# Hybrid SSD / RWKV-7 block on one core: high and low activations in one 512-column matmul of the input projection, rows normalised before the transposes

## The chip, the core and the metric

The kernel runs on one core of a Trainium2 chip. The core has a matmul engine (TensorE, PE in the profile; its weight loads are PEld) and four others that work beside it: VectorE (DVE), ScalarE (ACT), GpSimd (POOL) and the queue engine SyncE (SP), which here only issues DMAs. Each engine works through its own instructions in order, and semaphores make one wait for another. Matmuls write to PSUM, a small accumulation memory that the kernel uses as eight banks, each with room for 128 partitions x 512 f32; DVE and ACT read it from there. The metric is the time of one execution on the device, in microseconds (us).

## The reference

One layer of a streaming encoder block for 256 frames of 2048 channels, everything float32:

```python
u = rms_norm(h, norm1_g)                     # u = h * rsqrt(mean(h*h)) * g, by row (frame)
P = u @ w_in                                 # 2048 x 11744: z | x,B,C of the SSD | dt | r,k,v,wd,ad,gd of RWKV-7
pr = pr + (prev(pr) - pr) * rwkv_mu          # token shift: mixes each frame with the one before
y_ssd  = ssd_mixer(z, silu(conv4(xbc)), dt)  # Mamba-2, chunks of 64 frames
y_rwkv = rwkv7_mixer(r, k, v, wd, ad, gd)    # 32 heads of 64
h = h + concat(y_ssd, y_rwkv) @ w_out
v = rms_norm(h, norm2_g)
h = h + (silu(v @ w_gate) * (v @ w_up)) @ w_down      # D_FF = 5632
out = rms_norm(h, norm_f_g)
```

## The kernel before

**Products in three parts.** Every large product of float32 matrices is made of three faster ones. `split` turns a weight tile `raw` into a rounded high part `whi` (ACT, line 192) and the rest `wlo` (DVE, line 193); the activations have a high part `uh` and a low part `ul` in the same way. A product is then whi·uh + whi·ul + wlo·uh, added up in PSUM.

**Two kinds of product.** `gemm_a` makes 256 output channels x 256 frames with the weights as the stationary operand and the activations as the moving one: 16 slices of the 2048 input channels, two halves `b` of 128 output channels, and three matmuls of 256 columns for each (lines 277, 278, 279), 96 in all. It serves the low-rank inputs (`ps_l0`, `ps_l1`), r, k and v of eight RWKV pairs of 256 channels (`ps_rkv`, 24 calls), B and C (`ps_bc`, 4) and x of the SSD (`ps_xs`, 8): 38 calls. `gemm_b` turns the operands round: the activations are stationary and 512 weight columns move (lines 298 to 300). It serves z, the output projection (`add_out`, `ps_o`) and the FFN.

**PSUM.** Pool `mm` has four buffers of one bank for the results of both kinds; a `gemm_a` takes one, a `gemm_b` two (one for each half of the frames). Pool `mx`, four further banks, serves everything small. A buffer is given again only when the instructions that read its last result are done.

**Normalisation.** The raw x is transposed (line 247) and scaled by the norm weights into `uh`, `ul` (lines 252, 254). The factor of each frame, `rstd`, is not yet known then. It is worked out beside that (`square`, `finish`), spread over all partitions as a row `R` by a matmul (`row_scale`), and each `gemm_a` result is multiplied by R afterwards, in PSUM (`scaled`, line 231, DVE). z gets the factor in its activation. At the start the four quarters of x and the four weight tiles of `ps_l0` are loaded in turn, and the function `first` makes transposes, splits and matmuls quarter by quarter.

**After each gemm_a.** For r, k, v the function `shift` reads each half `j` of the scaled result twice: line 353 (ACT) writes a part to SBUF, line 354 (DVE) adds the frame before. B, C and x go through `conv` (line 877 on ACT, three times line 879 on DVE).

**Order.** Work beside the large products is put into a queue with due times (`Side`; one tick for each weight tile), and the framework's scheduler then places the instructions of each engine by priority, so the order on the engines is fixed at build time. The loop over the eight pairs makes k, v and r of pair `pi`, while the side queue has the recurrence of the two pairs before; then, from pair 3 on, `out_rwkv` multiplies the finished pair `pi - 3` with its 256 rows of the output projection: `add_out`, four column blocks n0 to n3 of 12 matmuls each, and each block is added to `h` by two DVE additions (line 311). B and C follow, then the output of pair 5, then four SSD groups g0 to g3 (two `ps_xs`, an `add_out` of another pair or group, one `ps_z` each), the last outputs, and the FFN, which takes the time from about 1112 us on.

Of the kernel before, what the change touches and what calls it, by code (L numbers as in the profile page):

```python
# [68 lines left out]
def tile_hybrid_block(ctx: ExitStack, tc: tile.TileContext, x, norm1_g, w_in, conv_w, conv_b, dt_bias, A_log, D_skip,  # L69
# [12 lines left out]
    mm = ctx.enter_context(tc.tile_pool(name="mm", bufs=4, space=PS))  # L82
# [5 lines left out]
    def mmt(name):  # L88
        return mm.tile([P, 2, T], F32, name=name, tag="mm")
# [23 lines left out]
    for _ in range(10):  # L113
        nc.tensor.matmul(ps[:, :P], ones, ones, start=True, stop=True)
# [81 lines left out]
    uh = ul = R = None  # L196
# [20 lines left out]
    def row_scale(i, pool):  # L217

        nonlocal R
        ps = mxt("ps_R")  # L220
        for b in range(2):
            r = finish(i, b)
            dg = pool.tile([P, P], F32, name="diag_r")
            nc.vector.tensor_scalar(dg, ident, r, None, ALU.mult)
            nc.tensor.matmul(ps[:, b * P:(b + 1) * P], ones, dg, start=True, stop=True)
        R = const.tile([P, T], F32, name="R")
        nc.scalar.copy(R, ps[:, :T])

    def scaled(ps):

        nc.vector.tensor_tensor(ps, ps, R.unsqueeze(1).broadcast_to([P, 2, T]), ALU.mult)
        return ps

    def to_channels(n, gcol, order=lambda ins: ins):

        nonlocal uh, ul
        if n == 0:
            uh = big.tile([P, KT, T], F32R, name="uh")
            ul = big.tile([P, KT, T], F32R, name="ul")
        tiles = []  # L240
        for k2 in range(2):
            ps = mxt("ps_n").rearrange("p (a t) -> p a t", a=2)
            tiles.append(ps)
            for b in range(2):
                for j in range(2):
                    c = n * 512 + (2 * k2 + j) * P
                    order(nc.tensor.transpose(out=ps[:, j, b * P:(b + 1) * P], in_=h[:, b, c:c + P], identity=ident))

        def half(k2):
            ks = [(4 * n + 2 * k2 + j, tiles[k2][:, j]) for j in range(2)]  # L250
            for k, ps in ks:
                order(nc.scalar.activation(uh[:, k], ps, AF.Copy, scale=gcol[:, k:k + 1]))
            for k, ps in ks:
                order(nc.vector.scalar_tensor_tensor(ul[:, k], ps, gcol[:, k:k + 1], uh[:, k].bitcast(F32), ALU.mult,
                                                     ALU.subtract))

        return half
# [9 lines left out]
    def gemm_a(w, cols, name, units=None):  # L267
        ps = mmt(name)
        for k0 in range(0, KT, 4):
            hi, lo = split(load_a(w, cols, k0)) if units is None else units(k0 // 4)  # L270
            for k in range(4):
                kt = k0 + k
                first, last = kt == 0, kt == KT - 1
                for b in range(2):
                    o = ps[:, b]
                    wh, wl = hi[:, k, b * P:(b + 1) * P], lo[:, k, b * P:(b + 1) * P]
                    nc.tensor.matmul(o, wh, uh[:, kt], start=first and b == 0, stop=False)  # L277
                    nc.tensor.matmul(o, wh, ul[:, kt], start=False, stop=False)  # L278
                    nc.tensor.matmul(o, wl, uh[:, kt], start=False, stop=last and b == 1)  # L279
            side.tick()  # L280
        return ps

    def gemm_b(w, r0, c0, acts, name):

        ps = [mmt(name).rearrange("p a t -> p (a t)") for _ in range(2)]
# [31 lines left out]
    cols = [(0, 256, CGD)]  # L317
    raws, halves = [], []
# [3 lines left out]
    halves.append(to_channels(0, colN, pin))  # L322

    def first(n):
        halves[n](0)
        hi_lo = split(raws[n], pin)
        halves[n](1)
        if n < 3:
            halves.append(to_channels(n + 1, colN, pin))
        for b in range(2):  # L330
            square(0, init, b, n, ("act", "vec")[b], pin)
        return hi_lo

    ps_l0 = gemm_a(w_in, cols, "ps_l0", first)
    row_scale(0, init)
# [32 lines left out]
    ps = scaled(ps_l0)  # L368
# [488 lines left out]
    for pi in range(8):  # L857
# [23 lines left out]
    for i in range(4):  # L881
        ps = scaled(gemm_a(w_in, [(0, 256, CXBC + 2048 + i * 256)], "ps_bc"))
        if i == 0:
# [3 lines left out]
            BC = bcp.tile([P, 2, 4, T], F32, name="BC")  # L887
        for j in range(2):
# [112 lines left out]
    uacts = [(uh[:, k], ul[:, k]) for k in range(KT)]  # L1001
    for g in range(4):
        xc = []
        for i in range(2):
            ps = scaled(gemm_a(w_in, [(0, 256, CXBC + g * 512 + i * 256)], "ps_xs"))
            t = xz.tile([P, 2, T], F32, name="xc", tag=f"xc{i}")
            for j in range(2):
                conv(t[:, j], ps[:, j], 4 * g + 2 * i + j)
# [8 lines left out]
        for b in range(2):  # L1017
            nc.scalar.activation(zs[:, b], psz[b], AF.Silu, scale=rstd[0][:, b:b + 1])
# [11 lines left out]
    def after(b, n):  # L1030
        square(1, npool, b, n, ("act", "vec")[b])
        if b == 1:
            half = to_channels(n, colB[:, N2:N2 + KT])
# [13 lines left out]
    uacts = [(uh[:, k], ul[:, k]) for k in range(KT)]  # L1047
# [97 lines left out]
```

## Time and profile before

| | |
|---|---|
| Runs | 1672.49, 1672.7 and 1674.29 us; median 1672.7 |
| Profiled execution | 1674.88 us, span of its instructions 1673.2 us, granted TensorE clock 0.999 |
| PE busy | 1654.7 us (99%), 12386 matmul records |
| PEld busy | 1440.8 us (86%) |
| DVE busy | 1196.1 us (71%) |
| ACT busy | 892.7 us (53%) |
| First matmul of `ps_l0`, of the first `ps_rkv` | 9.71 us, 37.81 us |

Busy time is a sum over stages. In the RWKV stage (37.8 to about 600 us) DVE is nearly as busy as PE; in the FFN PE stands alone. A difference of 2 us in 1674 between the profiled execution and the median is what separate executions of this kernel differ by (the runs above span 1.8 us).

### The profile page before, as it was taken

The page shows a single profiled execution, that of the slowest core. Times are in us where ns is not written, and L with a number is a line of the kernel's source. Part 1 is how long each engine was busy: PE and PEld are TensorE (multiplying, and loading weights), DVE is VectorE, ACT ScalarE, POOL GpSimd, SP SyncE. Part 2 cuts the span into 40 slices and gives each one's busy share as a digit, 9 for nine tenths or more (in the row PEclk, how much of TensorE's full clock was granted, in tenths as well). Part 3 has the DMA queues.
Part 4 walks back from the last instruction along what each step waited for, and adds up shares of the span by engine and source line. Part 5 has one row for each costly group of instructions (what it writes and reads, how often), then busy time and mean ns, then how long its engine had stood idle before and what let it go on. Part 6 is the DMA issues. An engine that isn't in the chain of part 4 may idle for free.

```text
span 1673.2 us, 30550 instructions
## 1 busy us (share of the span) xinstructions
PE 1654.7 (99%) x12386; PEld 1440.8 (86%) x12386; DVE 1196.1 (71%) x1859; ACT 892.7 (53%) x1390; POOL 18.0 (1%) x57
## 2 busy tenths in 40 slices
PE   8999999999999999999999999999999999999997
PEld 8999989899898998998988888888888888888886
DVE  7898889888888867978777746465565564554657
ACT  6655765765656456667565644444444444444444
POOL 3000000000000000000000000000000000000000
PEclk9999999999999999999999999999999999999999
DMA  8654445545455455665654666666666666666663
GB/s 256 173 147 117 131 127 147 145 121 148 119 150 146 121 171 182 204 209 157 177 171 152 204 192 190 194 190 189 191 190 197 186 193 191 189 189 197 190 190 126
DMA packets 212685, 286.91 MB, mean 171 GB/s; under 512 B 34978, under 2 KB 117696, under 8 KB 211904
## 3 DMA queue, kind: packets, MB, share of 16 engines
q1 hardware_dynamic: 211216, 282.67, 57.9%
q8 instruction: 97, 1.59, 0.4%
q0 software_dynamic: 752, 1.24, 0.3%
q10 hardware_dynamic: 576, 1.05, 0.2%
q14 instruction: 44, 0.36, 0.1%
HBM read 281.75 MB, written 3.18 MB: 170 GB/s over the span
## 4 chain that ended last, share of the span: by engine, by line
PE 73%; DVE 1%; DMA 0%; ACT 0%; issue 0%; DVEq 0%; SPq 0%
PE ps_o L298 8%; PE ps_o L300 7%; PE ps_o L299 7%; PE ps_gt L300 5%; PE ps_gt L298 5%; PE ps_up L299 5%; PE ps_gt L299 5%; PE ps_up L300 5%; PE ps_up L298 5%; PE ps_xs L277 2%; PE ps_xs L279 2%; PE ps_xs L278 2%; PE ps_z L300 2%; PE ps_z L299 2%; PE ps_z L298 2%; PE ps_bc L277 1%
## 5 line engine op out<-in xcount | busy, mean ns | idle before, releaser
L193 DVE TENSOR_TENSOR wlo<-raw,whi 128x1024 fp32r<-128x1024 f32 x508 | 620.2, 1221 | 373.9 <-ACT whi L192 372.2
L192 ACT CAST whi<-raw 128x1024 fp32r<-128x1024 f32 x508 | 532.9, 1050 | 623.5 <-PE ps_o L300 150.7
L277 PE MATMUL ps_rkv<-uh,whi 128*128 128x256 f32 x768 | 224.5, 292 | 0.0
L279 PE MATMUL ps_rkv<-uh,wlo 128*128 128x256 f32 x768 | 218.5, 285 | 0.7 <-DVE wlo L193 0.7
L278 PE MATMUL ps_rkv<-ul,whi 128*128 128x256 f32 x768 | 218.3, 284 | 0.0
L277 PEld LDWEIGHTS ps_rkv<-uh,whi 128*128 128x128 f32 x768 | 146.7, 191 | 5.5 <-issue 1.4
L279 PEld LDWEIGHTS ps_rkv<-uh,wlo 128*128 128x128 f32 x768 | 146.8, 191 | 1.7 <-DVE wlo L193 0.9
L278 PEld LDWEIGHTS ps_rkv<-ul,whi 128*128 128x128 f32 x768 | 146.8, 191 | 0.6
L298 PE MATMUL ps_gt<-whi,uh 128*128 128x512 f32 x352 | 137.1, 390 | 0.0
L299 PE MATMUL ps_gt<-wlo,uh 128*128 128x512 f32 x352 | 137.0, 389 | 0.0
L300 PE MATMUL ps_gt<-whi,ul 128*128 128x512 f32 x352 | 137.0, 389 | 0.0
L298 PE MATMUL ps_up<-whi,uh 128*128 128x512 f32 x352 | 136.9, 389 | 0.0
L299 PE MATMUL ps_up<-wlo,uh 128*128 128x512 f32 x352 | 136.9, 389 | 0.0
L300 PE MATMUL ps_up<-whi,ul 128*128 128x512 f32 x352 | 136.9, 389 | 0.0
L298 PE MATMUL ps_o<-whi,ah 128*128 128x512 f32 x336 | 131.7, 392 | 0.0
L300 PE MATMUL ps_o<-whi,al 128*128 128x512 f32 x336 | 130.9, 390 | 0.0
L299 PE MATMUL ps_o<-wlo,ah 128*128 128x512 f32 x336 | 130.7, 389 | 0.0
L311 DVE TENSOR_TENSOR h<-ps_o,h 128x512 f32<-128x512 f32 x184 | 120.0, 682 | 2.6 <-PE ps_o L300 2.2
L298 PE MATMUL ps_o<-whi,yh 128*128 128x512 f32 x256 | 105.7, 415 | 0.0
L299 PE MATMUL ps_o<-wlo,yh 128*128 128x512 f32 x256 | 100.2, 392 | 0.0
L300 PE MATMUL ps_o<-whi,yl 128*128 128x512 f32 x256 | 99.8, 394 | 0.0
L298 PEld LDWEIGHTS ps_up<-whi,uh 128*128 128x128 f32 x352 | 66.1, 188 | 13.7
(335 smaller groups left out, 3014.7 us busy)
## 6 DMA issues: line engine op xcount, KB each, us to landing
raw<-in_w_in_dram SPq DMA_DIRECT2D x180, 512.0 KB, 3.8
raw<-in_w_gate_dram SPq DMA_DIRECT2D x88, 512.0 KB, 3.8
raw<-in_w_up_dram SPq DMA_DIRECT2D x88, 512.0 KB, 3.7
raw<-in_w_down_dram SPq DMA_DIRECT2D x88, 512.0 KB, 4.6
raw<-in_w_out_dram SPq DMA_DIRECT2D x64, 512.0 KB, 4.4
csb<-cs_d SPq DMA_DIRECT2D x4, 1024.0 KB, 6.9
h<-in_x_dram SPq DMA_DIRECT2D x4, 512.0 KB, 7.5
g2s<-in_rwkv_g_dram SPq DMA_DIRECT2D x8, 256.0 KB, 3.5
```

The source lines that it names most:

```text
L192: order(nc.scalar.copy(hi, raw))
L193: order(nc.vector.tensor_tensor(lo, raw, hi.bitcast(F32), ALU.subtract))
L277: nc.tensor.matmul(o, wh, uh[:, kt], start=first and b == 0, stop=False)
L278: nc.tensor.matmul(o, wh, ul[:, kt], start=False, stop=False)
L279: nc.tensor.matmul(o, wl, uh[:, kt], start=False, stop=last and b == 1)
L298: nc.tensor.matmul(ps[b], ah[:, s], hi[:, k], start=first, stop=False)
L299: nc.tensor.matmul(ps[b], ah[:, s], lo[:, k], start=False, stop=False)
L300: nc.tensor.matmul(ps[b], al[:, s], hi[:, k], start=False, stop=last)
L311: nc.vector.tensor_tensor(d, ps[b], d, ALU.add)
```

## The change

1. `uh` and `ul` become one tile `ua`, with the high and the low part of each slice side by side. In `gemm_a` one matmul of 512 columns (line 258) makes whi·uh and whi·ul, into the two halves of a whole bank `ps[:, b]`; a second of 256 columns (line 260) adds wlo·uh to the low half. So 64 matmuls stand for 96.
2. The two halves are added by the new `add_low`: ACT copies the low half to the SBUF tile that will hold the result (`dst`, line 268), DVE adds it to the high half in PSUM (line 269). `shift` and `conv` then read as before.
3. A `gemm_a` result now has two banks. Pool `mm` has two buffers of two banks in place of four of one. A `gemm_b` takes one of these two for both halves.
4. All of x is loaded first; squares and `rstd` come next; the rows are scaled to `hn` (lines 315 on ACT, 316 on DVE), and `hn` is transposed. `R`, `scaled` and the scale of z go. The weights of `ps_l0` are loaded behind x, and `ps_l0` is an ordinary `gemm_a`. 30 warm-up matmuls (line 114) in place of 10.

```diff
-    mm = ctx.enter_context(tc.tile_pool(name="mm", bufs=4, space=PS))
+    mm = ctx.enter_context(tc.tile_pool(name="mm", bufs=2, space=PS))
...
-        return mm.tile([P, 2, T], F32, name=name, tag="mm")
+        return mm.tile([P, 2, 2, T], F32, name=name, tag="mm")
...
-    for _ in range(10):
+    for _ in range(30):
         nc.tensor.matmul(ps[:, :P], ones, ones, start=True, stop=True)
...
-    def gemm_a(w, cols, name, units=None):
+    def gemm_a(w, cols, name, dst=None, full=False):
...
-                    nc.tensor.matmul(o, wh, uh[:, kt], start=first and b == 0, stop=False)
-                    nc.tensor.matmul(o, wh, ul[:, kt], start=False, stop=False)
-                    nc.tensor.matmul(o, wl, uh[:, kt], start=False, stop=last and b == 1)
+                    nc.tensor.matmul(ps[:, b].rearrange("p a t -> p (a t)"), wh,
+                                     ua[:, kt].rearrange("p a t -> p (a t)"), start=kt == 0, stop=False)
+                    nc.tensor.matmul(ps[:, b, 1], wl, ua[:, kt, 0], start=False, stop=kt == KT - 1)
             side.tick()
-        return ps
+        if full:
+            return ps
+        add_low(ps, dst)
+        return ps[:, :, 0]
+
+    def add_low(ps, dst):
+        nc.scalar.copy(dst, ps[:, :, 1])
+        nc.vector.tensor_tensor(ps[:, :, 0], ps[:, :, 0], dst, ALU.add)
 
     def gemm_b(w, r0, c0, acts, name):
 
-        ps = [mmt(name).rearrange("p a t -> p (a t)") for _ in range(2)]
+        pt = mmt(name)
+        ps = [pt[:, b].rearrange("p a t -> p (a t)") for b in range(2)]
...
     for n in range(4):
         nc.sync.dma_start(out=h[:, :, n * 512:(n + 1) * 512], in_=xv[:, :, n * 512:(n + 1) * 512])
-        raws.append(load_a(w_in, cols, 4 * n))
...
+    for n in range(4):
         for b in range(2):
             square(0, init, b, n, ("act", "vec")[b], pin)
...
-    ps_l0 = gemm_a(w_in, cols, "ps_l0", first)
-    row_scale(0, init)
+    hn = init.tile([P, 2, D], F32, name="hn")
+    r0 = [finish(0, b) for b in range(2)]
+    for n in range(4):
+        c = slice(n * 512, (n + 1) * 512)
+        pin(nc.scalar.activation(hn[:, 0, c], h[:, 0, c], AF.Copy, scale=r0[0]))
+        pin(nc.vector.tensor_scalar(hn[:, 1, c], h[:, 1, c], r0[1], None, ALU.mult))
+        f = to_channels(n, colN, hn, pin)
+        f(0)
+        f(1)
...
         for i, (n, c) in enumerate((("k", CK), ("v", CV), ("r", CR))):
-            ps = scaled(gemm_a(w_in, [(0, 256, c + pi * 256)], "ps_rkv"))
             t = pp.tile([P, 2, T], F32, name="rkv", tag="t" + n, bufs=1)
+            ps = gemm_a(w_in, [(0, 256, c + pi * 256)], "ps_rkv", t)
```

The other calls of `gemm_a` (`ps_l0`, `ps_l1`, `ps_bc`, `ps_xs`) lose `scaled` and get a `dst` in the same way.

**How the instructions move.** The first place is the end of pair 3's r and the output projection that follows it. In these rows "waits DVE_49" is a semaphore that DVE raises. On PE, before, from the last small work ahead of block n2 (`ps_g`, the gate) to n2's two halves:

```order
L815 MATMUL ps_g<-gd_t,g2s 128x256 x3
L298 MATMUL ps_o<-whi,yh 128x512 [waits DVE_49,Activation_49]
L299 MATMUL ps_o<-wlo,yh 128x512
L300 MATMUL ps_o<-whi,yl 128x512
L298 MATMUL ps_o<-whi,yh 128x512 [waits DVE_49]
```

The same on PE after the change, from the last three matmuls of block n1 (lines 287 to 289 are the old 298 to 300) to the first of n2:

```order
L287 MATMUL ps_o<-whi,yh 128x512
L288 MATMUL ps_o<-wlo,yh 128x512
L289 MATMUL ps_o<-whi,yl 128x512
L662 MATMUL ps_b<-XT,t1s 32x32 [waits Activation_49] x2
L662 MATMUL ps_b<-XT,t1s 32x32 x14
L711 MATMUL ps_r<-vt,atk 64x64 [waits PE_49]
L711 MATMUL ps_r<-vt,atk 64x64 x3
L722 MATMUL ps_w<-rs,XF 64x64 [waits Activation_49]
L722 MATMUL ps_w<-rs,XF 64x64 x2
L287 MATMUL ps_o<-whi,yh 128x512 [waits DVE_49]
```

Before, n2 waited for the additions of n0 to `h`, and only n3 went into the bank of r. Now n2 takes the buffer of r, so its wait is for the last instruction that reads r, line 338 (the old 354) for half j=1; and four `ps_r` and three `ps_w` matmuls of the recurrence, which stood behind the whole output before, stand ahead of it.

On ACT, before, in the same place, from the first `shift` instruction of r (line 353) on; the small copies are of the recurrence (`ktt`, `t1s`) and of its group norm (`Y`):

```order
L353 ACTIVATE rkv<-ps_rkv,omA 128x256 [waits DVE_49]
L192 CAST whi<-raw 128x1024 [waits DMAHW3_49]
L567 COPY ktt<-tmp_4250 32x8x32 [waits DVE_49]
L567 COPY ktt<-tmp_4250 32x8x32 x3
L797 ACTIVATE Y<-Y,mv 128x64 [waits DVE_49]
L797 ACTIVATE Y<-Y,mv 128x64 x7
L353 ACTIVATE rkv<-ps_rkv,omA 128x256 [waits DVE_49]
L704 COPY t1s<-ps_b 32x256 [waits PE_49]
```

And on ACT after, from the same small copies on (line 268 is the new copy of the low half, 337 the old 353):

```order
L782 ACTIVATE Y<-Y,mv 128x64 x2
L552 COPY ktt<-tmp_2878 32x8x32 [waits DVE_49]
L552 COPY ktt<-tmp_2878 32x8x32 x3
L782 ACTIVATE Y<-Y,mv 128x64 x5
L268 COPY rkv<-ps_rkv 128x512 [waits PE_49]
L689 COPY t1s<-ps_b 32x256 [waits PE_49]
L689 COPY t1s<-ps_b 32x256
L192 CAST whi<-raw 128x1024 [waits DMAHW7_49]
L337 ACTIVATE rkv<-ps_rkv,omA 128x256 [waits DVE_49]
L192 CAST whi<-raw 128x1024 [waits DMAHW1_49]
L192 CAST whi<-raw 128x1024 [waits DMAHW3_49,PE_49]
L337 ACTIVATE rkv<-ps_rkv,omA 128x256 [waits DVE_49]
```

The first ACT instruction that reads r stood ahead of the copies `ktt` and the eight `Y`; its successor, the copy of the low half, stands behind them, and three weight casts stand between it and the second line 337.

The second place is the start. On DVE, before, from the first low parts of the activations (`ul`) on:

```order
L254 SCALAR_TENSOR_TENSOR ul<-ps_n,colN,uh 128x256 [waits PE_49,Activation_49]
L254 SCALAR_TENSOR_TENSOR ul<-ps_n,colN,uh 128x256
L193 TENSOR_TENSOR wlo<-raw,whi 128x1024 [waits DMAHW2_49,Activation_49]
L254 SCALAR_TENSOR_TENSOR ul<-ps_n,colN,uh 128x256 [waits PE_49,Activation_49]
L254 SCALAR_TENSOR_TENSOR ul<-ps_n,colN,uh 128x256
L207 SCALAR_TENSOR_TENSOR sq_v,ssq_164<-h 128x512 [waits DMAHW1_49]
```

On DVE after, from the third square to the first low parts (`ua` from line 236 is the old `ul`):

```order
L207 SCALAR_TENSOR_TENSOR sq_v,ssq_184<-h 128x512 [waits DMAHW3_49,DVE_49]
L207 SCALAR_TENSOR_TENSOR sq_v,ssq_184<-h 128x512 [waits DMAHW4_49,DVE_49]
L193 TENSOR_TENSOR wlo<-raw,whi 128x1024 [waits DMAHW5_49,Activation_49]
L212 TENSOR_REDUCE rstd_187<-ssq_184 128x1 [waits DVE_49]
L193 TENSOR_TENSOR wlo<-raw,whi 128x1024 [waits DMAHW6_49,Activation_49]
L214 RECIPROCAL rstd_187<-rstd_187 128x1 [waits Activation_49]
L316 TENSOR_SCALAR hn<-h,rstd_187 128x512 [waits DVE_49]
L193 TENSOR_TENSOR wlo<-raw,whi 128x1024 [waits DMAHW7_49,Activation_49]
L193 TENSOR_TENSOR wlo<-raw,whi 128x1024 [waits DMAHW0_49,Activation_49]
L236 SCALAR_TENSOR_TENSOR ua<-ps_n,colN,ua 128x256 [waits PE_49,Activation_49]
```

The first low part of the activations, which the first matmul of `ps_l0` needs, stood first; now all four squares of its half, the scaling of the row block and all four weight splits of `ps_l0` stand ahead of it.

More of the change, by code (lines that the diff above doesn't have):

```diff
@@ L215, in finish, with to_channels @@
         return r
[L217 to L231, printed above, removed]
-        return ps
-    def to_channels(n, gcol, order=lambda ins: ins):
-        nonlocal uh, ul
+    def to_channels(n, gcol, src, order=lambda ins: ins):
+        nonlocal ua
         if n == 0:
-            uh = big.tile([P, KT, T], F32R, name="uh")
-            ul = big.tile([P, KT, T], F32R, name="ul")
+            ua = big.tile([P, KT, 2, T], F32R, name="ua")
         tiles = []
@@ L246, in to_channels @@
                     c = n * 512 + (2 * k2 + j) * P
-                    order(nc.tensor.transpose(out=ps[:, j, b * P:(b + 1) * P], in_=h[:, b, c:c + P], identity=ident))
+                    order(nc.tensor.transpose(out=ps[:, j, b * P:(b + 1) * P], in_=src[:, b, c:c + P], identity=ident))
         def half(k2):
@@ L251, in half @@
             for k, ps in ks:
[L252 removed]
+                order(nc.scalar.activation(ua[:, k, 0], ps, AF.Copy, scale=gcol[:, k:k + 1]))
             for k, ps in ks:
[L254 to L255 removed]
+                order(nc.vector.scalar_tensor_tensor(ua[:, k, 1], ps, gcol[:, k:k + 1], ua[:, k, 0].bitcast(F32),
+                                                     ALU.mult, ALU.subtract))
         return half
@@ L366, in tile_hybrid_block @@
     pp = pst.enter_context(tc.tile_pool(name="pp", bufs=1, side="right"))
-    ps = scaled(ps_l0)
+    ps = gemm_a(w_in, [(0, 256, CGD)], "ps_l0", gd_t)
     for j in range(2):
@@ L881, in tile_hybrid_block @@
     for i in range(4):
-        ps = scaled(gemm_a(w_in, [(0, 256, CXBC + 2048 + i * 256)], "ps_bc"))
+        pt = gemm_a(w_in, [(0, 256, CXBC + 2048 + i * 256)], "ps_bc", full=True)
         if i == 0:
@@ L999, in ssd_group @@
         return [prep, cbt, lmat(0), diag(0), state, post(0), lmat(1), diag(1), off, post(1)]
-    uacts = [(uh[:, k], ul[:, k]) for k in range(KT)]
+    uacts = [(ua[:, k, 0], ua[:, k, 1]) for k in range(KT)]
     for g in range(4):
@@ L1004, in tile_hybrid_block @@
         for i in range(2):
-            ps = scaled(gemm_a(w_in, [(0, 256, CXBC + g * 512 + i * 256)], "ps_xs"))
             t = xz.tile([P, 2, T], F32, name="xc", tag=f"xc{i}")
+            ps = gemm_a(w_in, [(0, 256, CXBC + g * 512 + i * 256)], "ps_xs", t)
             for j in range(2):
@@ L1017, in tile_hybrid_block @@
         for b in range(2):
-            nc.scalar.activation(zs[:, b], psz[b], AF.Silu, scale=rstd[0][:, b:b + 1])
+            nc.scalar.activation(zs[:, b], psz[b], AF.Silu)
         side.drain()
@@ L1032, in after @@
         if b == 1:
-            half = to_channels(n, colB[:, N2:N2 + KT])
+            half = to_channels(n, colB[:, N2:N2 + KT], h)
             half(0)
@@ L1046, in tile_hybrid_block @@
     nc.gpsimd.dma_start(out=gfb, in_=norm_f_g.partition_broadcast(P))
-    uacts = [(uh[:, k], ul[:, k]) for k in range(KT)]
+    uacts = [(ua[:, k, 0], ua[:, k, 1]) for k in range(KT)]
     def back(gt, ah, al):
```

30 lines of the change are left out of this document (11 added, 19 removed).

## The prediction

> **What bounds the kernel now.** I read the busy times and the slices of the page first, then a table by stretches, then the waits.
>
> ```profile
> PE 1654.7 (99%) x12386; PEld 1440.8 (86%) x12386; DVE 1196.1 (71%) x1859; ACT 892.7 (53%) x1390; POOL 18.0 (1%) x57
> PE   8999999999999999999999999999999999999997
> DVE  7898889888888867978777746465565564554657
> core 0: us, PE busy (x) PEld busy (x) DVE busy (x) ACT busy (x) POOL busy (x), PEclk, DMA share, GB/s
> 232.80:248.00 15.20, 15.20 (x188) 12.08 (x184) 14.14 (x27) 13.09 (x29) 0.00 (x0) 1.00 0.44 115
> 248.00:316.00 68.00, 67.99 (x843) 61.51 (x838) 60.09 (x115) 42.81 (x90) 0.55 (x3) 1.00 0.49 135
> ...
> PE ps_w L737 <- ACT rs L733: 1.8, 2, 1.0
> ```
>
> PE is busy in every slice but the first and last. A microsecond of matmuls saved is a microsecond of time, and a microsecond in which PE waits is one lost: nothing hides either. The first stretch, of 15.2 us, is one output projection in the RWKV stage (n0 to n3 in pair 3's turn), the second the three products of the next turn. In the first DVE works 14.14 and ACT 13.09 of 15.20 us, so anything PE has to wait for there stands in a full queue. PE waits almost nowhere at present: the last row, 1.8 us in two waits, is the largest entry of the list.
>
> **The matmuls.** Starts of neighbouring matmuls, from the timeline, give the pace of both widths:
>
> ```profile
> 326.44 0.28 PE L277 MATMUL ps_rkv<-uh,whi 128*128 128x256 f32 x1
> 326.56 0.28 PE L278 MATMUL ps_rkv<-ul,whi 128*128 128x256 f32 x1
> 326.68 0.28 PE L279 MATMUL ps_rkv<-uh,wlo 128*128 128x256 f32 x1
> ...
> 303.17 0.40 PE L298 MATMUL ps_o<-whi,yh 128*128 128x512 f32 x1
> 303.40 0.39 PE L299 MATMUL ps_o<-wlo,yh 128*128 128x512 f32 x1
> 303.63 0.39 PE L300 MATMUL ps_o<-whi,yl 128*128 128x512 f32 x1
> L277 PE MATMUL ps_rkv<-uh,whi 128*128 128x256 f32 x768 | 224.5, 292 | 0.0
> ```
>
> 256 columns take 120 ns, 512 take 227 to 230 (unrounded, 227). Three of 256 are 360; one of 512 and one of 256 are 347. So the wide form saves 13 ns for each of 768/24 = 32 groups, 0.43 us a call. The 36 calls behind the start (24 rkv, 4 bc, 8 xs) give -15.6 us; the two at the start are in its own term. The ends: -15.6, or nothing if the pair is held at 360 by its weight loads (a rival below).
>
> The Trainium skill, "TensorE: Matmul & The Clock Gate", section "Back-to-back issue gap", gives about 81 ns a matmul at 128 columns and 131 at 512 for a long stream. By it, with an estimate of 98 ns at 256 on the line between, a group would fall from 294 to 229 ns and 38 calls would gain an estimated 79 us. The 227 ns above contradict it for this data type, and I give that outcome no chance.
>
> **The new evacuation by itself.** DVE's addition (line 269) stands for its product with R (line 231), of the same 512 elements: taken at the same 687 ns, no difference. ACT gets a copy of 128x512 from PSUM for each call, by its nearest row 586 ns; 38 of them are 22 us on an engine busy 53%. Beside the matmuls both cost nothing; what they cost lies where PE waits for them.
>
> ```profile
> L231 DVE TENSOR_TENSOR ps_rkv<-ps_rkv,R 128x512 f32<-128x512 f32 x24 | 16.5, 687 | 0.9 <-PE ps_rkv L279 0.8
> L1057 ACT CAST ah<-ps_t 128x512 fp32r<-128x512 f32 x22 | 11.7, 586 | 0.0
> L311 DVE TENSOR_TENSOR h<-ps_o,h 128x512 f32<-128x512 f32 x184 | 120.0, 682 | 2.6 <-PE ps_o L300 2.2
> ```
>
> **Two buffers in place of four: the RWKV output stages.** These rows are of the first one; r's last matmul is the first of them.
>
> ```profile
> 231.55 0.28 PE L279 MATMUL ps_rkv<-uh,wlo 128*128 128x256 f32 x1
> 235.14 0.47 ACT L353 ACTIVATE rkv<-ps_rkv,omA 128x256 f32<-128x256 f32 x1
> 236.58 1.65 ACT L567 COPY ktt<-tmp 32x256 f32<-32x256 f32 x4
> 238.24 2.77 ACT L797 ACTIVATE Y<-Y,mv 128x64 f32<-128x64 f32 x8
> 240.91 0.45 ACT L353 ACTIVATE rkv<-ps_rkv,omA 128x256 f32<-128x256 f32 x1
> 241.40 0.48 DVE L354 SCALAR_TENSOR_TENSOR rkv<-ps_rkv,colA,rkv 128x255 f32<-128x255 f32 x1 [0.66 <-ACT rkv L353]
> 242.17 2.01 ACT L192 CAST whi<-raw 128x1024 fp32r<-128x1024 f32 x2
> 241.69 0.58 PE L298 MATMUL ps_o<-whi,yh 128*128 128x512 f32 x1
> 248.06 0.39 PE L277 MATMUL ps_rkv<-uh,whi 128*128 128x256 f32 x1
> ```
>
> r is read to the end only at 241.88, 10 us after its last matmul, because ACT's queue is full of the recurrence. PE didn't care: n2, at 241.69, used other banks. Now n2 takes r's buffer. With these durations in the new order of ACT: the last Y ends near 239.5, the copy at 240.1, DVE's addition at 240.9; t1s (0.75) and a weight cast (1.05) put the first line 337 at 241.9 to 242.35. DVE, past a weight split (1.22, which waits for that cast), has its half at 243.6; two casts later ACT makes the second line 337 at 244.9, the XF copies and the copy `rs` (for which `ps_w`, now ahead of n2 on PE, waits) at 245.9. So n2 starts near 246.1. Ahead of it, n1 waits for both of n0's additions, the second behind a Y product on DVE: 0.8. n3 (for n1's additions) and the next k (for n2's) find their buffers free. The next k then starts near 251.6 in place of 248.06; 0.4 of that is the moved `ps_r` and `ps_w`, done later before. +3.1 for each of the five stages (pairs 3 to 7): **+15.5**. Ends: if ACT kept its old order, n2 would wait to 241.9 plus the added instruction, 0.8 a stage, +4; with every queue as late as it could be, 4.6, +23. I take the chain, since the order is fixed in the program and both queues are full there.
>
> **The same, with B, C and the SSD groups.** Where consecutive blocks of an `add_out` share a buffer, PE stops between them for two additions of 682 ns and whatever DVE has ahead of them:
>
> ```profile
> 700.51 0.69 DVE L311 TENSOR_TENSOR h<-ps_o,h 128x512 f32<-128x512 f32 x1
> 701.36 0.16 DVE L984 RECIPROCAL ss<-ss 128x1 f32<-128x1 f32 x1 [0.16 <-ACT ss L983]
> 701.44 0.67 DVE L311 TENSOR_TENSOR h<-ps_o,h 128x512 f32<-128x512 f32 x1
> 702.03 0.47 DVE L879 SCALAR_TENSOR_TENSOR xc<-ps_xs,colC,xc 128x255 f32<-128x255 f32 x1
> ...
> 763.61 1.28 ACT L983 ACT_TABLE_LOAD   x1
> 766.17 1.28 ACT L1009 ACT_TABLE_LOAD   x1
> ```
>
> Here the additions (of which the four of two blocks take 700.51 to 705.16) alternate with the conv's. After B and C, n1 and n2 both follow in one buffer: two waits of about 2, **+4** (2 to 6). In g0 other matmuls fill the gap, 0. In g1 again two, +3.5. In g2 and g3 n1 follows n0 in one buffer while ACT has two table loads, a cast and the new copy before the conv lets DVE go on: 3.5 each. Together **+10** (4 to 13). In the later outputs and the FFN the two buffers alternate, and a block of 24 matmuls or more (5.4 us) covers two additions: 0 (to +0.5).
>
> **The start.**
>
> ```profile
> h<-in_x_dram SPq DMA_DIRECT2D x4, 512.0 KB, 7.5
> 8.00:10.00 2.00, 1.11 (x10) 1.14 (x11) 1.94 (x4) 2.00 (x6) 1.44 (x4) 1.00 1.09 367
> 1.13 4.64 PE L114 MATMUL ps_up<-ones 128*128 128x128 f32 x20 [1.13 <-DVE eps L105]
> 8.89 1.06 PE L247 MATMUL ps_n<-ident,h 128*128 128x128 f32 x8 [1.64 <-DMA h<-in_x_dram]
> 8.66 1.23 DVE L193 TENSOR_TENSOR wlo<-raw,whi 128x1024 fp32r<-128x1024 f32 x1
> 9.71 0.36 PE L277 MATMUL ps_l<-uh,whi 128*128 128x256 f32 x1
> 37.81 0.28 PE L277 MATMUL ps_rkv<-uh,whi 128*128 128x256 f32 x1
> L207 DVE SCALAR_TENSOR_TENSOR sq_v<-h 128x512 f32<-128x512 f32 x8 | 5.5, 686 | 0.0
> ```
>
> At 0.367 MB/us the 2.1 MB of x are in near 10.2, the weight tiles at 11.8, 13.2, 14.7 and 16.1. 30 warm-up matmuls last to about 10 (60 records, the first 20 at 0.23, later ones at the 0.11 to 0.13 of the transposes), and the norm weights, which DVE copies ahead of its squares, come behind them. Then DVE in its new order: four squares with their read-outs to about 14, two splits (2 x 1.22) and the second rstd to 16.7, a row block (0.5), two more splits to 19.7, `ua`: the first matmul of `ps_l0` near 20, 10.3 later than now. From there PE has two calls (22.2 us) and the transposes (about 2.6) without the gaps of now: 25 to 27.5 to the first `ps_rkv`, near 46 where it was 37.81: **+8**. Ends +5 and +11.
>
> PE does nothing from about 10 to 16 but a few transposes. The Trainium skill ("TensorE: Matmul & The Clock Gate", "The HAM clock gate") lets the clock fall to half after some 3.4 us without work, which would make an estimated 2 us of those 8; the gap of 1.64 above cost no clock, and no longer one is in this trace.
>
> **Sum.** -15.6 + 15.5 + 4 + 10 + 8 = +21.9 on 1674.9, so 1696.8; this execution stands 2.2 above the median, so **1694.5** against 1672.7. All low ends give 1672, all high ends 1710, both against the median.
>
> **Rivals.**
> *The evacuations are in time* (the other side). If ACT and DVE run far enough ahead that each buffer is free within 0.3 us of PE's asking, the 11 places cost 3 in all and the sum is -15.6 + 3 + 8: 1668, faster. For it: in the second stretch of the table ACT works 43 of 68 us. Against it: in the output stages both are full, and r's rows show 10 us. It decides where all waits together stay under 4 us. 0.16.
> *A quarter of the waits* (7.5 in place of 29.5): -15.6 + 7.5 + 8 is 0, 1672.7. For it: the low ends of the waits add up to 10. 0.12.
> *The clock falls in the new waits.* The same page, in "A second HAM failure mode: psum-queue depth-cycling", tells of clocks lost in short pauses between groups that cycle through PSUM. As a mechanism here: after a wait of 4 us the next 3.4 us of matmuls run at half pace, 1.7 us for each of 11 waits, +19: 1713. Against it, the granted clock is 1.00 in every stretch, though with no such waits. 0.06.
> *Loads hold the pace.* If 120 ns is the time of a weight load and not of 256 columns, and a pair takes 360, the saving goes: 1710. Against it: both widths stand 13 ns above a common slope (107 ns for 256 columns), as streams do. 0.05.
> *As summed*: 0.61; its own range is 1682 to 1706.
>
> **Numbers.** What can be told from no change is 0.2%, 3.3 us. Faster is the first rival and a sliver of the sum's low end, 0.17; same 0.12; slower 0.71. The range leaves out part of the first rival, and the highest two cases: 1667 to 1708.
>
> **What would show it.** The matmuls of lines 258 and 260 every 227 and 120 ns. PE idle, ended by DVE's line 338, ahead of `ps_o` in five stages, about 3 us each; by DVE's line 300 six times between 590 and 850; PE busy down from 99% to about 97%. First `ps_l` near 20, first `ps_rkv` near 46. It fails if the waits on line 338 are under 1 us (ACT reached its copy early), if the first `ps_rkv` comes before 42, or if the pair of matmuls does not take 347.

## The result and the profile after

The changed kernel takes 1722.22 us (median of four runs, 1718.46 to 1723.44) against 1673.49: ratio 1.0286, 95% interval 1.0266 to 1.0306. It is slower by 2.9%, where 1694.5 was forecast (+1.3%) with a range up to 1708. The profiled execution has a span of 1721.7 us, 48.5 more than before.

Busy times and the clock's slices, from the page of the changed kernel, and then the three largest waits of PE from its list of waits (total us, count, longest):

```profile
PE 1671.7 (97%) x11206; PEld 1385.6 (80%) x11206; DVE 1201.9 (70%) x1861; ACT 915.8 (53%) x1433; POOL 19.5 (1%) x57
PEclk8999999999999999999999999999999999999999
```

```profile
PE ps_w L722 <- ACT rs L718: 12.7, 7, 2.2
PE ps_o L287 <- DVE h L300: 10.7, 5, 3.4
PE ps_n L229 <- ACT hn L315: 5.5, 1, 5.5
```

PE does 1180 matmul records fewer and is busy 17 us longer. That can't be explained by waits, which are idle time: the matmuls that are left must be slower. The granted clock says why: 0.985 on average, 0.999 before; a slice of 43 us is too coarse to show it. Where the 48.5 us arise, from the starts of the stages in both timelines:

| stage | before, us | after, us | difference |
|---|---|---|---|
| up to the first `ps_rkv` | 37.81 | 47.30 | +9.5 |
| k, v, r of pairs 0 to 3 | 194.99 | 197.31 | +2.3 |
| five output stages, pairs 3 to 7 | 77.29 | 104.49 | +27.2 |
| the four turns of k, v, r between them, and B, C | 278.67 | 270.81 | -7.9 |
| output behind B and C, groups g0 to g3 | 291.66 | 306.76 | +15.1 |
| later outputs and the FFN, to the last product | 772.48 | 772.63 | +0.2 |
| the last product (`ps_f`) to the end | 20.30 | 22.43 | +2.1 |

**The start.** PE in the changed kernel:

```profile
16.06 0.69 PE L229 MATMUL ps_n<-ident,hn 128*128 128x128 f32 x2 [5.46 <-ACT hn L315]
19.79 0.80 PE L258 MATMUL ps_l<-ua,whi 128*128 128x512 f32 x1 [1.33 <-DVE ua L236]
47.30 0.40 PE L258 MATMUL ps_rkv<-ua,whi 128*128 128x512 f32 x1
```

The first matmul of `ps_l0` comes at 19.79 (forecast 20), and its 0.80 us, twice a usual 0.40, is the first sign of the clock.

**The first output stage** in the changed kernel, engines mixed, from the work ahead of r's evacuation on ACT to the end of the stage (r's last matmul ended near 243.5):

```profile
249.87 1.77 ACT L782 ACTIVATE Y<-Y,mv 128x64 f32<-128x64 f32 x5
251.54 0.57 ACT L268 COPY rkv<-ps_rkv 128x512 f32<-128x512 f32 x1
254.99 0.45 PE L711 MATMUL ps_r<-vt,atk 64*64 64x64 f32 x8
256.25 0.47 ACT L337 ACTIVATE rkv<-ps_rkv,omA 128x256 f32<-128x256 f32 x1
256.75 0.48 DVE L338 SCALAR_TENSOR_TENSOR rkv<-ps_rkv,colA,rkv 128x255 f32<-128x255 f32 x1
257.67 0.44 PE L722 MATMUL ps_w<-rs,XF 64*64 64x64 f32 x6 [2.23 <-ACT rs L718]
258.05 0.50 PE L287 MATMUL ps_o<-whi,yh 128*128 128x512 f32 x1
259.44 0.63 PE L288 MATMUL ps_o<-wlo,yh 128*128 128x512 f32 x1
259.87 0.63 PE L289 MATMUL ps_o<-whi,yl 128*128 128x512 f32 x1
262.27 0.39 PE L289 MATMUL ps_o<-whi,yl 128*128 128x512 f32 x1
262.50 0.39 PE L287 MATMUL ps_o<-whi,yh 128*128 128x512 f32 x1
```

The chain of the prediction is there link by link: the copy behind the Y work, line 337 behind three casts, line 338 at 256.75, 13.3 us after r's last matmul (it was 10 before). PE stands 2.23 us, and n2 starts 13.45 us after the stage's first matmul, where the chain had 13.3. What follows is new: from 259.0 to 261.6 matmuls start every 0.43 us in place of 0.23. The table by stretches has the granted clock (the column behind POOL) of these moments:

```profile
core 0: us, PE busy (x) PEld busy (x) DVE busy (x) ACT busy (x) POOL busy (x), PEclk, DMA share, GB/s
255.40:258.60 3.20, 0.97 (x10) 0.79 (x9) 3.03 (x6) 3.12 (x8) 0.00 (x0) 1.00 0.70 173
258.60:262.00 3.40, 3.40 (x10) 2.61 (x8) 2.42 (x3) 1.30 (x3) 0.00 (x0) 0.51 0.01 4
262.00:265.20 3.20, 3.20 (x15) 2.67 (x14) 2.50 (x4) 1.06 (x1) 0.12 (x1) 0.99 0.60 164
```

Ten matmul starts in 3.40 us at half clock, fifteen in 3.20 us at full clock; "busy" reads the same in both. The clock's record holds such stretches of 3.41 us at half clock in each of the five output stages (a double one in the third), after one wait each in g1, g2 and g3, and two in pair 1: 11 units, 37.5 us, some 18.8 us lost (half of it, as PE works through nearly all). One of 10.2 us lies in the start, with `ps_l0` at work in the last 3.4 us of it. In the kernel before there is none up to its last 5 us.

The widest pauses of the changed kernel after the start are not in the output stages but in g2 and g3, where n1 follows n0 in one buffer; and the last product, whose blocks share buffers too, waits once more:

```profile
804.36 0.47 PE L287 MATMUL ps_o<-whi,yh 128*128 128x512 f32 x1 [3.38 <-DVE h L300]
1711.33 0.50 PE L1086 MATMUL ps_f<-dhi,ah 128*128 128x512 f32 x1 [0.93 <-DVE h L1090]
```

**The pace of the pairs.**

```profile
769.92 0.28 PE L260 MATMUL ps_xs<-ua,wlo 128*128 128x256 f32 x1
770.04 0.40 PE L258 MATMUL ps_xs<-ua,whi 128*128 128x512 f32 x1
770.27 0.28 PE L260 MATMUL ps_xs<-ua,wlo 128*128 128x256 f32 x1
770.38 0.40 PE L258 MATMUL ps_xs<-ua,whi 128*128 128x512 f32 x1
```

A wide one takes 230 to 241 ns here (medians of all starts: 232 in `ps_xs`, 235 in `ps_rkv`), a narrow one 117: 349 to 352 a pair, where 347 was counted.

### The profile page after: what moved, and what is told of

Same layout as the page of the kernel before. It is cut to its first block, busy times and chain, and to the rows that moved or that the text cites. A ratio compares the mean times of both kernels' runs of the same rounds, so it can differ in the third digit from the quotient of the medians.

```text
span 1721.7 us, 28220 instructions
## 1 busy us (share of the span) xinstructions
PE 1671.7 (97%) x11206; PEld 1385.6 (80%) x11206; DVE 1201.9 (70%) x1861; ACT 915.8 (53%) x1433; POOL 19.5 (1%) x57
## 4 chain that ended last, share of the span: by engine, by line
PE 85%; ACT 6%; DVE 6%; DMA 2%; issue 1%; DVEq 0%; SPq 0%; ACTq 0%
PE ps_o L287 7%; PE ps_o L289 7%; PE ps_o L288 7%; PE ps_rkv L258 7%; PE ps_gt L287 5%; PE ps_up L288 5%; PE ps_gt L288 5%; PE ps_up L287 5%; PE ps_gt L289 5%; PE ps_up L289 5%; PE ps_rkv L260 4%; PE ps_xs L258 3%; PE ps_a L570 2%; PE ps_bc L258 2%; ACT whi L192 2%; PE ps_xs L260 2%
## 5 line engine op out<-in xcount | busy, mean ns | idle before, releaser
L258 PE MATMUL ps_rkv<-ua,whi 128*128 128x512 f32 x768 | 283.2, 408 | 0.0
L260 PE MATMUL ps_rkv<-ua,wlo 128*128 128x256 f32 x768 | 218.6, 285 | 1.9 <-DVE wlo L193 1.9
L258 PEld LDWEIGHTS ps_rkv<-ua,whi 128*128 128x128 f32 x768 | 145.0, 189 | 36.2 <-issue 1.2
L260 PEld LDWEIGHTS ps_rkv<-ua,wlo 128*128 128x128 f32 x768 | 146.2, 190 | 3.8 <-DVE wlo L193 2.3
L288 PE MATMUL ps_gt<-wlo,ua 128*128 128x512 f32 x352 | 137.0, 389 | 0.0
L287 PE MATMUL ps_gt<-whi,ua 128*128 128x512 f32 x352 | 137.0, 389 | 0.0
L289 PE MATMUL ps_gt<-whi,ua 128*128 128x512 f32 x352 | 137.0, 389 | 0.0
L287 PE MATMUL ps_up<-whi,ua 128*128 128x512 f32 x352 | 136.9, 389 | 0.0
L288 PE MATMUL ps_up<-wlo,ua 128*128 128x512 f32 x352 | 136.9, 389 | 0.0
L289 PE MATMUL ps_up<-whi,ua 128*128 128x512 f32 x352 | 136.9, 389 | 0.0
L258 PE MATMUL ps_xs<-ua,whi 128*128 128x512 f32 x256 | 91.2, 399 | 0.0
L287 PEld LDWEIGHTS ps_up<-whi,ua 128*128 128x128 f32 x352 | 66.1, 188 | 13.8
```

The costliest lines, as they stand in the source:

```text
L258: nc.tensor.matmul(ps[:, b].rearrange("p a t -> p (a t)"), wh, ua[:, kt].rearrange("p a t -> p (a t)"), start=kt == 0, stop=False)
L260: nc.tensor.matmul(ps[:, b, 1], wl, ua[:, kt, 0], start=False, stop=kt == KT - 1)
L287: nc.tensor.matmul(ps[b], ah[:, s], hi[:, k], start=first, stop=False)
L288: nc.tensor.matmul(ps[b], ah[:, s], lo[:, k], start=False, stop=False)
L289: nc.tensor.matmul(ps[b], al[:, s], hi[:, k], start=False, stop=last)
```

## The experiments

Three theories were set against each other. A: the two double buffers, with r's late evacuation, make PE wait, and the half clock follows the waits. B: two buffers alone are enough. C: the wide matmuls themselves bring the clock down. All runs but a probe of the pace (e13) in one table, each beside runs of the kernel before on the same chip:

| run | time, us | ratio to before (95%) |
|---|---|---|
| changed kernel | 1722.2 | 1.0286 (1.0266 to 1.0306) |
| e1_pool: before, two double buffers | 1690.4 | 1.0097 (1.0082 to 1.0112) |
| e2_start: before, new start | 1691.0 | 1.0102 (1.0087 to 1.0117) |
| e9_product: e2 and a DVE product | 1683.5 | 1.0057 (1.0042 to 1.0072) |
| e3_narrow: changed, narrow matmuls | 1699.3 | 1.0152 (1.0136 to 1.0167) |
| e4_warm: changed, start kept busy | 1718.7 | 1.0264 (1.0248 to 1.0279) |
| e5_early: changed, early evacuation | 1709.0 | 1.0204 (1.0187 to 1.0221) |
| e6_filler: changed, idle matmuls in the pause | 1706.6 | 1.0198 (1.0183 to 1.0213) |
| e7_three: changed, three double buffers | 1698.7 | 1.0150 (1.0134 to 1.0165) |
| e8_order: changed, other order of a slice | 1713.3 | 1.0232 (1.0215 to 1.0249) |
| e10_oldstart: changed, old start | 1710.1 | 1.0205 (1.0188 to 1.0222) |
| e11_adds: e5 and early additions | 1702.3 | 1.0169 (1.0153 to 1.0184) |

**Buffers alone.**

```diff
-    mm = ctx.enter_context(tc.tile_pool(name="mm", bufs=4, space=PS))
+    mm = ctx.enter_context(tc.tile_pool(name="mm", bufs=2, space=PS))   # tiles of two banks
...
-        ps = mmt(name)
+        ps = mmt(name)[:, 0]                                            # gemm_a; gemm_b as in the change
```

> The kernel before with nothing changed but the buffers: pool mm has two buffers of two banks, a narrow gemm_a uses one bank of its buffer, gemm_b one buffer. Theory A (buffers and late evacuation together make the waits, and the half clock follows the waits): r's evacuation keeps its old order and ends about when n2 asks, so each output stage loses about 1 us, B/C and g1 about 2 each; in all +5 to +12 us on 1673.5, clock 1.00 nearly everywhere. Theory B (two buffers alone do it): the waits of the changed kernel, +25 us or more, with half-clock stretches in the five output stages. Theory C (the wide matmuls themselves bring the clock down): 1673 to 1678, clock as before.

+16.8 us at clock 0.999: above A's price, well below B's. Output stages grow by 0.5 to 1.3 us each, the row of B, C and the groups by 6.3, and no half-clock stretch appears in any stage. Two rows of PE's waits:

```profile
PE ps_w L738 <- ACT rs L734: 6.1, 10, 1.1
PE ps_o L299 <- DVE ss L985: 2.5, 2, 1.3
```

None is longer than 1.3 us in the stages. So two buffers cost waits, but short ones; B falls, and A had the buffers too cheap.

**The new start alone**, and then with a DVE product put back that multiplies each result by one:

```diff
+        nc.vector.tensor_tensor(ps, ps, onesT.unsqueeze(1).broadcast_to([P, 2, T]), ALU.mult)   # e9_product only
```

> The kernel before with the new start alone: x first, rows normalised, no row R and no product with it, 30 warm-up matmuls; three narrow matmuls and four single banks as before. Theory A: the first ps_rkv comes near 47.5 in place of 37.8 and the rest is as before, +9 to +10 us: 1683. DVE is spared 38 products of 0.69 us, worth nothing where PE is the bound. Rival: that relief lets DVE run ahead and gives back 2 us or more: 1678 to 1681.

> The start-alone kernel (1691, +17.4, of which its trace has 9.6 at the start) with a DVE product of the old size (128x512 in PSUM, times ones) put back behind each gemm_a. Theory F (the other 7.8 us come from the new order in which the scheduler puts DVE's work once the product is gone): PE's waits for wlo and t1s in the RWKV stage go, 1683 to 1685. Rival G (they come from something else in the new start that lasts, such as the phase of weight loads): the product costs DVE 0.69 x 38 = 26 us more where it is nearly full, 1691 or more.

The start is worth what theory A said (first `ps_rkv` at 47.39 and 47.92), but e2 lost some 7 us more, nearly all in its five output stages (84.1 us together, 77.3 before), against both sides of its forecast, which had nothing or a gain there. Its waits, and then those of e9 after the start:

```profile
PE ps_rkv L262 <- DVE wlo L193: 4.3, 5, 1.3
PE ps_b L655 <- DVE t1s L668: 3.4, 5, 1.3
PE ps_o L282 <- DVE wlo L193: 2.7, 5, 0.6
```

```profile
PE ps_b L663 <- DVE t1s L676: 0.8, 1, 0.8
PE ps_rkv L270 <- DVE wlo L193: 0.5, 1, 0.5
```

With 21 us more busy time on DVE the kernel is 7.5 us faster, and the five stages take 77.6. The product isn't useful work; taking it out changed the order in which the scheduler places DVE's splits and small products (at the start of the first output stage `t1s` stands ahead of a `wlo` split in e9, as before, and behind it in e2), and PE came to wait for them. The start by itself is +9.0 us.

**The old start in the changed kernel** (R multiplied in behind `add_low`):

> The changed kernel with the old start (raw x quarter by quarter, row R, 10 warm-up matmuls); R is multiplied in by a DVE product behind add_low, so DVE does an addition and a product for each gemm_a. Theory A (start and waits add up): the first ps_rkv near 38, no half clock in the start, -9.5; the added DVE product lengthens r's evacuation by 0.7 and the waits by as much or less in five stages: 1713 to 1717. Rival: the late DVE turns 0.69 x 24 us in the RWKV stage into waits of PE: 1722 or more.

-12 us, a little more than forecast: the first `ps_rkv` comes at 39.08. The output stages, 19.8 to 22.9 us, are as long as in the changed kernel, so the late evacuation and the half clock don't hang on the new start. But PE's longest pauses there are shorter, 1.1 to 1.5 us between small products, and four of the five stages lost the clock behind them, as the first did from 241.88 to 248.71:

```profile
240.92 0.75 PE L681 MATMUL ps_b<-XT,t1s 32*32 32x32 f32 x64 [1.45 <-DVE t1s L694]
```

So the length of a pause isn't the whole rule; the last section has more.

**The start kept busy** by 26 idle matmuls in the gap:

> The changed kernel with 26 more warm-up matmuls behind the transpose of the norm weights, where PE is idle from 10.6 to 16 us. Theory A: the clock stays at 1.0 up to the first ps_l matmul, which still starts near 19.8; the 3.5 us that the first matmuls spend at half clock go, the first ps_rkv at 45 to 45.8 in place of 47.3, total -1.7 us on 1722. Rival (the clock falls for what the matmuls draw, not for the idle time): clock and first ps_rkv as in the changed kernel.

The clock is 1.00 from 10 to 30 us, but the first `ps_rkv` comes at 46.76, 0.5 earlier, not 1.7: from the first `ps_l` on the start is 1.5 shorter, while that first one slipped from 19.79 to 20.77 because a weight split on DVE waited for its cast on ACT. The 3.6 us that the median gained are more than that, but the two intervals overlap. The profiled execution, the fastest of the four, is 7.8 us shorter than that of the changed kernel; four units of half clock are missing in it behind the start, two of them in pair 1, although the pause of 1.94 us ahead of the second is the same. That is luck, which the last section takes up.

**Evacuation first.**

```diff
+        with tc.high_priority():
             nc.scalar.copy(dst, ps[:, :, 1])
             nc.vector.tensor_tensor(ps[:, :, 0], ps[:, :, 0], dst, ALU.add)      # shift in the same way
```

> The changed kernel with add_low and shift at the scheduler's highest priority: on ACT the copy of r's low half then stands ahead of the table load, the vt, ktt and Y work, and r's last reader ends some 4 us after r's last matmul in place of 13. Theory A: the wait of 2.2 us ahead of n2 and the 3.4 us at half clock behind it (1.7 us lost) go in all five stages, -15 to -20 us: 1702 to 1707; the waits of B/C and of the SSD groups stay. Theory C: the half-clock stretches stay although the waits go, at most -11. Rival D: the side work that is pushed back makes PE wait elsewhere by as much: 1715 or more.

-13.2 us, under the forecast of 15 to 20. The stage is what was foreseen, and the next turn isn't:

```profile
246.29:262.44 16.15, 15.58 (x190) 12.06 (x185) 14.85 (x29) 14.55 (x31) 0.00 (x0) 1.00 0.34 92
262.44:315.22 52.78, 52.21 (x556) 43.34 (x557) 45.79 (x87) 30.12 (x64) 0.56 (x3) 1.00 0.52 149
```

16.15 us in place of 20.6, all at full clock; but the turn of k, v, r takes 52.78 in place of 51.0, some of it small products that no longer stand in the output stage, some waits for casts that were pushed back.

**Idle matmuls in the pause.** The decisive run between A and C:

```diff
+                if c == 0 and 2 <= pi <= 6:                                   # in step_r, between ps_r and its copy
+                    pf = mxt("ps_up")
+                    for _ in range(10):
+                        tc.keep_in_program_order(nc.tensor.matmul(pf[:, :P], ones, ones, start=True, stop=True))
```

> The changed kernel with nine idle matmuls (ones x ones, 128 columns, about 2 us) on PE behind ps_r, where PE stands still for 2.2 us ahead of n2 in the five output stages; nothing that waits is changed, though ps_w comes to stand behind n2. The idle matmuls compute nothing that is used. Theory A (the half clock follows the pause): no half-clock stretch in the five stages, their length 20.6 to 18 or 18.9, total -8 to -12 on 1722. Theory C (the clock falls for what the matmuls draw): stretches of 3.4 us stay, the stages 20 us or more, total within 4 of 1722.

-15.6 us by added work (matmuls of ones, whose result nobody reads), more than the 8 to 12 expected. The first stage (a table by stretches) and its pause (the timeline):

```profile
241.59:259.98 18.39, 18.11 (x216) 14.29 (x210) 16.34 (x30) 15.91 (x35) 0.00 (x0) 1.00 0.33 85
```

```profile
252.36 2.27 PE L720 MATMUL ps_up<-ones 128*128 128x128 f32 x18
254.39 0.47 PE L287 MATMUL ps_o<-whi,yh 128*128 128x512 f32 x1
```

n2 starts no sooner than the buffer allows, yet all five stages take 18.4 us at clock 1.00, and the half clock is gone from them. The wide matmuls are the same as before and keep the full clock, so C falls. The five stages gained 12.5 us; another 3.2 lie in pairs 0 to 3 and 1.4 in the groups, where no work was added and three stretches of half clock are missing by luck. Part of the 2.2 to 3.5 us a stage is that n2 no longer stands behind `ps_w`; a stretch itself was worth 1.6, as e8 shows by chance: in its second stage the clock held after a pause of 2.25 us, in its third it fell.

```profile
313.88:332.95 19.07, 16.52 (x204) 12.76 (x199) 17.19 (x31) 16.07 (x35) 0.00 (x0) 1.00 0.35 91
383.54:404.21 20.67, 18.20 (x203) 13.94 (x199) 17.59 (x31) 16.05 (x35) 0.12 (x1) 0.92 0.36 97
```

**Another order of the slice** (wide, wide, narrow, narrow):

> The changed kernel with the four matmuls of a slice in another order: wide, wide, narrow, narrow in place of wide, narrow, wide, narrow. Measured in the changed kernel: a wide one takes 236 ns ahead of a narrow one, a narrow one 117 ahead of a wide one, 353 a pair, where the forecast had 347. Theory (a wide one costs 227 ahead of a wide one, and the narrow one hides the load of the next): the four take 227 + 236 + 120 + 117 = 700 in place of 706, total -3 to -4 us on 1722, within its noise. Rival (alternating sizes are what costs the 9 ns): 694, -6. Rival E (weight loads bound the narrow ones, and two in a row lose it again): 706 or more, 0 to +4.

Of its -9 some 5 are again the clock, three units fewer; the rest agrees with the 3 to 4 expected from the pace. That moved little (233 and 231 to 236 ns for the wide ones, 116 to 119 for the narrow: some 700 for the four, as the first theory said, but not by its 227).

**All matmuls wide**, as a probe of that pace (one run):

```diff
-                    nc.tensor.matmul(ps[:, b, 1], wl, ua[:, kt, 0], start=False, stop=kt == KT - 1)
+                    nc.tensor.matmul(ps[:, b].rearrange("p a t -> p (a t)"), wl,
+                                     ua[:, kt].rearrange("p a t -> p (a t)"), start=False, stop=kt == KT - 1)
```

> The changed kernel with the low weights' matmul 512 columns wide as well (it adds the product of the two low parts, which the others leave out): all matmuls of gemm_a are wide. A probe of the pace only. In the changed kernel a wide one starts 231 to 236 ns before the next, against 227 in gemm_b, and the forecast counted 227. Theory H (the narrow neighbour costs the 4 to 9 ns, its weight load being hidden less): all wide ones go to 227. Rival I (the operands do, moving ua in place of weights): they stay at 231 or more. Total, by 32 groups x 38 calls x 110 ns more, about +130 us on 1722.

1823.5 us, where some 1852 was expected, and the pace:

```profile
329.18 0.39 PE L260 MATMUL ps_rkv<-ua,wlo 128*128 128x512 f32 x1
329.40 0.39 PE L258 MATMUL ps_rkv<-ua,whi 128*128 128x512 f32 x1
329.63 0.39 PE L260 MATMUL ps_rkv<-ua,wlo 128*128 128x512 f32 x1
329.86 0.39 PE L258 MATMUL ps_rkv<-ua,whi 128*128 128x512 f32 x1
```

227 ns (the median in both stages). The same operands reach it once no narrow matmul is among them. So mixing widths costs a wide one 4 to 9 ns and gives a narrow one 3 back, 2 to 5 ns a pair net; that the weight load of the neighbour is the means of it was not shown. And with nothing but wide matmuls three units of half clock are left after the start, each behind a pause of 2.0 to 3.3 us: C falls here too.

**Narrow matmuls in the changed kernel**, without `add_low`:

> The changed kernel (new start, two double buffers, activations in one tile) with three narrow matmuls into one half again and no add_low: no wide matmul, no copy of the low half. If the parts add up, buffers alone (+16.8) and start alone (+17.4) give +34: 1707 to 1709, and the wide form with its evacuation carries the other 14. Theory A': the late copy on ACT is what turns waits of 1 us into 2.4 us and half clock; here r's evacuation ends some 10 us after r's last matmul, stages 17 to 18 us, no half-clock stretch in them. Theory B: stages and clock as in the changed kernel, 1722 to 1730.

1699.3, less than the sum of the parts (buffers +16.8, start +9.0, DVE's order +7.5 make +33; together they cost +25; the first and third may change the same order, which was not tested). The stages are 17.3 to 18.4 us, and no stretch at half clock comes after the start: as A' said. r is read to the end 12.4 to 13.5 us after its last matmul started (13.9 to 15.5 in the changed kernel), and PE waits 0.6 in the first stage and up to 0.8 in the others:

```profile
251.89 0.48 DVE L335 SCALAR_TENSOR_TENSOR rkv<-ps_rkv,colA,rkv 128x255 f32<-128x255 f32 x1
252.42 0.50 PE L284 MATMUL ps_o<-whi,yh 128*128 128x512 f32 x1 [0.63 <-DVE rkv L335]
```

So the wide form with its copy and addition makes the kernel 22.9 us slower than the narrow one in the same frame: it saves matmul time, and its longer evacuation turns waits of 0.6 to 0.8 us into ones of 2.2 that drop the clock.

**Three double buffers**, two banks for small products:

> The changed kernel with three double buffers for the large products and two single banks (before: four) for the small ones. Theory A: blocks n0, n1, n2 no longer wait for r's evacuation; stages of about 16 us, no half clock there, -20 to -25 us if the small products bear it. Rival D: with two banks the recurrence's small products wait for each other's evacuation and PE with them: more than 1722.

-23.6, as forecast, and by another road: stages of 15.8 us, but `ps_w` now waits in the turn of k, v, r, and the half clock moves there with it (0.97 on average). What the stages gained (25.4) the turns, with B and C, nearly gave back (22.7); 17 us came from the output behind B and C and the groups.

```profile
243.53:259.35 15.82, 15.72 (x190) 12.17 (x185) 14.48 (x27) 14.22 (x31) 0.00 (x0) 1.00 0.34 93
259.35:315.89 56.54, 53.74 (x561) 44.51 (x557) 46.50 (x89) 31.00 (x64) 0.61 (x3) 0.97 0.49 140
```

**Additions first as well:**

> The early-evacuation kernel (1709) with the additions of the output blocks to h at highest priority as well. In the changed kernel PE waits for the second addition 2.6 us in g1 and 3.4 in g2 and g3, each with 3.4 us at half clock behind it. Theory A: those waits shrink to the two additions themselves, 1.3 to 1.5 us, and at least two of the three half-clock stretches go: -6 to -10 on 1709, 1699 to 1703. Rival (the additions wait for PE or ACT and not for their place in DVE's queue): 1707 to 1711.

1702.3, -6.7 on e5: in g2 and g3 the pause shrinks from 3.38 to 2.54 and still drops the clock; in g1 it is 1.75 and the clock holds. So one stretch of the three went, where theory A had at least two; 2.9 us lie in pairs 0 to 3, where the clock held after a pause of 2.35 us behind which it had fallen in e5. None of these versions beats the kernel before. Combinations were not run, but the wide form has some 10 us to give, and the start alone takes 9.

## Why the prediction was wrong

The direction and most links held; the size failed, by the clock. The step that failed is in the sum: it has no term for the clock behind the waits, because "The clock falls in the new waits" was set aside as a rival with a chance of 0.06. It is not a rival but a consequence of the forecast's own waits. Against it I had set that the granted clock is 1.00 in every stretch of the profile before, and had noted that this trace has no such waits: a row that can't speak on the question. Its price was right, in part by luck: it had +19 for 11 waits of 4 us, and measured are 11 units of half clock, 18.8 us, but behind waits of 1.4 to 3.4; two units lie in pair 1, where no wait was forecast, one stage has a double one, and the waits behind B and C have none. Had it stood in the sum, the forecast would have been 1713, 9 us from the result.

Term by term, against the profiled execution:

- *Start, +8*: +9.5, and +9.0 by itself (e9). The first matmul at 19.79 for 20; the half clock in the gap, which the prediction took from the Trainium skill ("TensorE: Matmul & The Clock Gate", "The HAM clock gate") as an estimated 2 us, is there with 0.64 from 10 to 20 us and cost about 1.5 (e4).
- *Matmuls, -15.6*: a pair takes 349 to 352, not 347, so 8 to 11 ns a group in place of 13: -9 to -13. (13 ns on 1152 groups are 15.0; 15.6 was rounded up on the way.) The pace was put together from two uniform streams; the mixture has its own, as e13 shows.
- *Output stages, +15.5*: with the turns behind them 27.2 - 7.9 = +19.3; their 16 calls saved some 4.5, so the waits cost about 24, of which 10.2 are half clock (six units of 1.7). The waits proper, about 13.5, are the forecast's: it had a stage at 18.8 us, and one in which the clock held took 19.07 (e8).
- *B, C and groups, +4 and +10*: +15.1 with what the matmuls saved. Block by block the output behind B and C grew by 3.7, that of g0 by 0.6, those of g1, g2 and g3 by 5.3 each, of which 1.7 are half clock: 3.7, 0.6 and 3.6 without it, where 4, 0 and 3.5 were forecast.
- *Later outputs and FFN, 0 to +0.5*: +0.2 up to the last product, but that one was overlooked: its blocks take one buffer for two, PE waits 0.93 and 0.33 us, +2.1 to the end. e1 has the same, e2 not.
- *Pairs 0 to 3*, in no term of their own: +2.3 where 12 calls save 3 to 4; two half-clock units (3.4) and short waits for DVE.

Most of what the forecast said would show it, did: `ps_o` late in five stages, PE at 97%, 19.79 and 47.30 at the start, line 300 at the end of five waits (it had six). Three details were off. The pair of matmuls did not take 347, which the forecast had named as a sign of failure. PE's wait was put down to line 338, and it ended with the copy `rs`, 0.4 us later, as the working itself had it. And it is 2.2 us of idle time, not 3.

The other rivals: the evacuations were not in time, nor were the waits a quarter of what was counted; loads did not hold the pair at 360. No stream of wide matmuls had a median pace under 227 ns (e13), so the gain of 79 us that the prediction gave no chance did not come either.

## What to carry to other kernels

A wait that a change brings onto a saturated TensorE is not paid once: add the clock behind it, here 1.7 us for nearly every pause of 2.2 us or more and for some shorter ones, and take "the clock is full now" as no evidence while the kernel has no pauses. Before widening a result tile, list what must have read the buffer that the next product takes, and where that reader stands in its engine's queue; halving the number of buffers put an evacuation that ended 10 us late, harmless before, onto the path. And build a mixed stream's pace from a mixed stream: 2 to 5 ns on 1152 groups were 15 to 40% of the gain.

## What the runs showed of the hardware

The clock's stretches at half speed are 3.41 us long or a multiple, and start at multiples of 3.41 us from each other in one execution (258.7, 330.3, 402.0, 477.1 and 548.8 us in the changed kernel: 21, 21, 22 and 21 times). So whether a pause drops the clock depends on how it lies to that grid as well as on its length. By length alone it is unclear: pauses of 3.3 to 3.4 us dropped it 12 times of 12 and the 15 of 2.2 us in output stages 14 times, but 2.83 us (e10) did so once of twice, and 1.43 us (e7) five times of five.

Counted step by step of the grid, from 30 to 1600 us, the fourteen traces (the kernel before, the changed one and its variants) fall apart better. The boundaries were read from these traces afterwards; no run was made to test them.

| idle time of PE within one step of 3.41 us at full clock | clock fell at the end of the step |
|---|---|
| 1.94 us or more | 33 of 33 |
| 1.35 to 1.93 us, with ten or more small matmuls (32 or 64 rows) | 13 of 13 |
| 1.35 to 1.93 us, otherwise | 1 of 14 |
| less | 0 of 6325 |

So a pause counts by the part of it that lies in one step, and light work beside it counts towards it: that is how e7 and e10 lost the clock behind short pauses, and why the same pause of 1.94 us lost it in the changed kernel and not in e4. The Trainium skill ("TensorE: Matmul & The Clock Gate", "The HAM clock gate") describes a free-running window of about 3.4 us, which the grid agrees with; pauses of 2.2 us, shorter than the window, were enough here. This may also explain the wider spread of the changed kernel's runs, 5 us for 1.4 to 3 before, since the stretches of the pauses near 2 us come and go between executions: the clock of its four runs is 0.984 to 0.989, and the fastest has the highest.
